# A hybrid attention and Mamba-2 decoder layer: TensorE order written out from the start, products of queries and keys moved inside the attention beats, and 128-row operands in the last SSD chunk

## The chip, the cores and the metric

The kernel runs on one core of a Trainium2 chip. A core has TensorE (PE, matrix products into the PSUM accumulators), VectorE (DVE), ScalarE (ACT) and GpSimd (POOL) for elementwise work, SyncE (SP), which here issues all transfers, and 16 DMA engines. The metric is the device time in microseconds (us) of one execution. A difference under about 0.3% (5.8 us) can't be told from no change here.

## The reference

One layer of a decoder trunk serves a prompt (1 sequence of 1024 tokens) and a sample group (8 sequences of 8 new tokens, with a cache), 1088 tokens in all, in float32.

```python
mod = silu(c) @ w_ada + b_ada                  # shift, scale, gate of each sequence
h = rmsnorm(x, norm_g) * (1 + scale) + shift
q, k, v, g_att, z, xbc, dt, g_a, g_b = split(h @ w_in)
# 3 groups of 8 heads of 64: windows (128, 1), (512, 4), (2048, 16), ALiBi
o_g, lse_g = dilated_attention(q_g, k_g, v_g); att = combine(o_g, lse_g)
y = ssd(silu(conv(xbc)), dt, chunk=128)        # within a sequence: 8 chunks; samples: one of 8 tokens
y = group_rmsnorm((y + d_skip * x) * silu(z))
merged = sigmoid(g_a) * (att * silu(g_att)) @ w_att + sigmoid(g_b) * y @ w_ssm
out = rmsnorm(x + gate * (merged @ w_out))
```

## The kernel before

Activations are stored transposed: 128 features in the partitions, the 1088 tokens in the free dimension, 8 such tiles for the 1024 features. Products with `w_in` are made in three passes (`whi` with `h_hi`, `wlo` with `h_hi`, `whi` with `h_lo`), each in token chunks of 368, 368 and 352. The products of attention and SSD are plain float32, which the trace shows as two records for each matmul; a transpose is one record.

**The opening stage** (pool `ph0`). `xT` is loaded and squared; `sums` adds the squares over the partitions on TensorE, `rms` turns them into reciprocal roots, and four small matmuls `rb` spread these over all partitions. `ada(q)`, for q = 0 to 3, loads two blocks `wa` of `w_ada` (1 MB each), multiplies them with the conditioning vector (L316, four column blocks of 32), copies the result to `row` (ScalarE, L318), transposes it (`adaT`, L320) and makes from it the scale and shift `mod` of the feature tiles 2q and 2q+1 (VectorE, L327 to L329). `modulate(f)` then makes `h_hi[f]` and `h_lo[f]`: for the prompt's 1024 columns VectorE L338, ScalarE L339, VectorE L341; for the 64 sample columns GpSimd L335 to L337, ScalarE L340, GpSimd L342. The first two projections (keys and queries of the first head pair, `early`) are made tile by tile as `h` comes: `passes` goes over two feature tiles at a time, first the two passes with `h_hi`, then that with `h_lo`.

In this stage a planner orders every engine's queue by program order and by its own estimate of when things are ready. From `region` on (behind this stage) TensorE's queue is kept in program order (`manual_schedule`), and the other engines' queues are still the planner's.

**The attention stage.** While the projections `pj` run on, `Order` counts TensorE's time and lets in pieces of attention when they are due. `prompt_group` handles one of 12 pairs (hp = 0 to 3, g = 0 to 2) in beats. A beat i has up to three parts on TensorE: `values(i-2)` (tile `o`, values times transposed weights, 128 rows by 64 columns of the array), `turned(i-1)` (tile `pt`, transposes of the weights `pr`, all of the array), and `scores(i)` (tile `s`, queries times keys, 64 rows by 128 columns). Behind the scores, VectorE (L617) adds the mask and takes the maximum and ScalarE (L620) makes the exponents, both in `pr`, of which there is one buffer. For g = 0 and 1 there are 4 blocks (nb = 4), for g = 2 there are 2:

```python
for i in range(nb + 2):
    if i > 1:
        values(i - 2)
    if 0 < i <= nb:
        turned(i - 1)
    if i < nb:
        scores(i)
```

**The SSD stage** works in the same manner beside the other projections. In `x_tile` the tile `yd` holds the products within a chunk; the ninth chunk (c = 8) has the 64 sample tokens, and its matmuls read 64 rows of `xdt` and of the decay tile `mt` (L1075). The rows 64 to 127 of `mt` for these columns are products with rows of `CB` that are set to zero (L933).

Of the kernel before, what the change touches and what calls it, by code (L numbers as in the profile page):

```python
# [18 lines left out]
NB = 8  # L19
# [91 lines left out]
def trunk(ctx: ExitStack, tc: tile.TileContext, I, O):  # L111
# [36 lines left out]
    def P(name):  # L148
        a, n = PACK[name]
        return pack[:, a:a + n]  # L150
# [73 lines left out]
            SP.dma_start(out=o, in_=i)  # L224
        del copies[:n]

    def passes():

        for ks in (range(i, i + 2) for i in range(0, KO, 2)):
            for k in ks:  # L230
                yield k, 0, 0
                yield k, 1, 0
            for k in ks:
                yield k, 0, 1

    def project_early(js, ws, banks):

        ps = [[b[i](f"early{n}") for i in range(3)] for n, b in enumerate(banks)]
        for k, a, b in passes():
            for w, p in zip(ws, ps):  # L240
                for (c0, cn), q in zip(CHUNKS, p):
                    PE.matmul(q[:, :cn], w[a][:, k, :], (h_hi, h_lo)[b][k][:, c0:c0 + cn], start=(k, a, b) == (0, 0, 0),
                              stop=(k, a, b) == (KO - 1, 0, 1))
        for j, p in zip(js, ps):
            early[j] = p

    loaded = {}

# [40 lines left out]
        return I["w_in"][j]  # L289


    with pool("ph0", 2) as p0:
        xT = [p0.tile([128, TT], F32, name=f"xT{k}", bufs=1) for k in range(KO)]
        cT = p0.tile([128, 8, 9], F32, name="cT", bufs=1)
        SP.dma_start(out=cT, in_=I["cT"])
        for k in range(KO):
            SP.dma_start(out=xT[k], in_=I["xT"][k])
        SP.dma_start(out=pack, in_=I["pack"])
        cth = p0.tile([128, 8, 9], F32, name="cth", bufs=1)
        S.activation(cth, cT, AF.Tanh, scale=0.5)  # L300
        V.scalar_tensor_tensor(cth, cth, 1.0, cT, op0=OP.add, op1=OP.mult)
        V.tensor_scalar_mul(scT[:, :, :9], cth, 0.5)
        mod = p0.tile([128, 2, 8, 9], F32, name="mod", bufs=1)
        bs = p0.tile([128, 8], F32, name="bs", bufs=1)
        V.tensor_scalar_add(bs, P("b_ada")[:, 8:], 1.0)

        def ada(q):

            pr = bankB("ada")
            for k in range(0, 8, 4):  # L310
                wa = p0.tile([128, 4, 4, 128], F32, tag="wa", name="wa", bufs=6)
                SP.dma_start(out=wa.rearrange("p k j n -> p k (j n)"),
                             in_=I["w_ada"][q, k:k + 4].rearrange("k p n -> p k n"))
                for i in range(4):
                    for j in range(4):
                        PE.matmul(pr[j * 32:j * 32 + 32, :128], scT[:, k + i, :], wa[:, i, j, :], start=k + i == 0, stop=k + i == 7)  # L316
            row = p0.tile([128, 128], F32, tag="row", name="row")
            S.activation(row, pr[:, :128], AF.Copy)  # L318
            pt = bankB("adaT")
            PE.transpose(pt[:, :128], row, ident)  # L320
            fs = slice(2 * q, 2 * q + 2)
            pt = pt[:, :128].rearrange("p (i c n) -> p i c n", i=2, c=2)

            def each(ap):
                return ap[:, fs, None].to_broadcast([128, 2, 9])

            V.tensor_tensor(mod[:, 1, fs, :], pt[:, 1, :, :9], each(bs), op=OP.add)  # L327
            V.tensor_tensor(mod[:, 1, fs, :], mod[:, 1, fs, :], each(P("norm_g")), op=OP.mult)
            V.tensor_tensor(mod[:, 0, fs, :], pt[:, 0, :, :9], each(P("b_ada")), op=OP.add)  # L329

        def modulate(f):
            h = xT[f]
            hs = h[:, T:].rearrange("p (b s) -> p b s", b=NB)
            shift = mod[:, 0, f, 0:1]
            G.tensor_tensor(h[:, T:], h[:, T:], rb[:, T:], op=OP.mult)  # L335
            G.tensor_tensor(hs, hs, mod[:, 1, f, 1:, None].to_broadcast([128, NB, NS]), op=OP.mult)
            G.tensor_tensor(hs, hs, mod[:, 0, f, 1:, None].to_broadcast([128, NB, NS]), op=OP.add)  # L337
            V.scalar_tensor_tensor(h[:, :T], h[:, :T], mod[:, 1, f, 0:1], rb[:, :T], op0=OP.mult, op1=OP.mult)  # L338
            S.activation(h_hi[f][:, :T], h[:, :T], AF.Identity, bias=shift)  # L339
            S.activation(h_hi[f][:, T:], h[:, T:], AF.Copy)  # L340
            V.scalar_tensor_tensor(h_lo[f][:, :T], h[:, :T], shift, h_hi[f][:, :T].bitcast(F32), op0=OP.add, op1=OP.subtract)  # L341
            G.tensor_tensor(h_lo[f][:, T:], h[:, T:], h_hi[f][:, T:].bitcast(F32), op=OP.subtract)  # L342

        with tc.high_priority():
            ps = bankA("ms")
            for k in range(KO):
                s2 = p0.tile([128, TT], F32, tag="sqk", name="sqk")
                S.activation(s2, xT[k], AF.Square)
                sums(ps, s2, k == 0, k == KO - 1)
            ms = p0.tile([128, 3, QT], F32, name="ms", bufs=1)  # L350
            rms(ms, ps, D)
            rb = p0.tile([128, TT], F32, name="rb", bufs=1)
            for j in range(4):
                ps = (bankPJ if j < 3 else bankC)("rb")
                row = slice(j * 32, j * 32 + 1)
                PE.matmul(ps[:, :QT], onesc[row, :], ms[row, 1, :], start=True, stop=True, tile_position=(j * 32, 0))
                if j % 2:
                    V.tensor_copy(rb[:, j * QT:(j + 1) * QT], ps[:, :QT])
                else:
                    S.activation(rb[:, j * QT:(j + 1) * QT], ps[:, :QT], AF.Copy)  # L360
        js = (J_K, J_Q)
        for q in range(4):
            ada(q)
            if q == 0:
                ws = [load_w(w_in(j), KO, 128, wp, soon=0)[:2] for j in js]
            for f in (2 * q, 2 * q + 1):
                modulate(f)
        project_early(js, ws, ([bankPJ] * 3, [bankA, bankA, bankC]))


    dsk = const.tile([32, 4], F32, name="dsk")
# [106 lines left out]

        return ap.rearrange("p (r i) -> p i r", r=DIL[g])

    region = ctx.enter_context(ExitStack())
    region.enter_context(tc.manual_schedule(engines={mybir.EngineType.PE}))
    with ExitStack() as actx:
        ap_ = actx.enter_context(pool("att", 2))
        a1 = actx.enter_context(pool("att1", 1))
# [104 lines left out]
        def prompt_group(hp, g, n, q, k, v, msk, o):  # L590
# [3 lines left out]
            per = 512 // w  # L594
            nb = 8 // per
            st = ap_.tile([128, 2, 2, 8], F32, tag="st", name="st")
            prs, pTs, pos = {}, {}, {}

            def behind(u):
                return 2 if (g == 0 and u > 0) or (g == 1 and u % 2 == 1) else 1  # L600
# [1 line left out]
            def scores(i):  # L602
                us = range(i * per, i * per + per)

                ps = [bankA("s0"), bankA("s1")]
                for u in us:
                    nkb = behind(u)
                    c0, k0 = (u - us[0]) * w, (u + 1 - nkb) * 128
                    for h in range(2):
                        hs = slice(h * 64, h * 64 + 64)  # L610
                        mm(ps[h][:, c0:c0 + nkb * 128], q[hs, u * 128:(u + 1) * 128], k[hs, k0:k0 + nkb * 128], 110.0 * nkb,
                           start=True, stop=True)
                pr = prs[i] = ap_.tile([128, 2, 512], F32, tag="pr", name="pr", bufs=1)
                for u in us:
                    c0, m = (u - us[0]) * w, behind(u) * 128
                    for h in range(2):
                        V.tensor_tensor_reduce(out=pr[:, h, c0:c0 + m], in0=ps[h][:, c0:c0 + m], in1=msk[:, h, w - m:w],  # L617
                                               scale=-1.0, scalar=3e38, op0=OP.add, op1=OP.min,
                                               accum_out=st[:, 0, h, u:u + 1])
                        S.activation(pr[:, h, c0:c0 + m], pr[:, h, c0:c0 + m], AF.Exp, scale=-1.0,  # L620
                                     bias=st[:, 0, h, u:u + 1], accum_out=st[:, 1, h, u:u + 1])
# [41 lines left out]
            for i in range(nb + 2):  # L663
                if i > 1:
                    values(i - 2)
                if 0 < i <= nb:
                    turned(i - 1)
                if i < nb:
                    scores(i)
                if i == nb - 1:  # L670
                    order.passed.add(("s", n))
                if i <= nb:
# [148 lines left out]
    with ExitStack() as bctx:  # L821
# [136 lines left out]
        def x_tile(gr, xt, Bk, Bs, CB, CT, CS, sq):  # L958
# [108 lines left out]
            for q in range(3):  # L1067
# [4 lines left out]
                for c in range(4 * q, 4 * q + 4 if q < 2 else 9):  # L1072
                    n = 128 if c < 8 else TS
                    for h in range(2):
                        mm(ps[h * 64:h * 64 + 64, (c % 4) * 128:(c % 4) * 128 + n],  # L1075
                           xdt[:n, c, h * 64:h * 64 + 64], mt[h][:n, c * 128:c * 128 + n], 115.0, start=True, stop=True)
                V.tensor_add(u[:, 512 * q:512 * q + w], u[:, 512 * q:512 * q + w], ps[:, :w])
            V.scalar_tensor_tensor(u, u, 0.5, tiles.pop(("z", xt)), op0=OP.mult, op1=OP.mult)
            SP.dma_start(out=u_d[xt], in_=u)
# [278 lines left out]
```

## Time and profile before

| what | value |
|---|---|
| median of 3 runs | 1927.37 us (1922.1 to 1928.04) |
| the profiled execution's own time | 1927.42 us |
| its span, first to last instruction | 1925.6 us |
| TensorE busy | 1866.4 us (97%) |
| VectorE busy | 1065.8 us (55%) |
| ScalarE busy | 644.9 us (33%) |
| GpSimd busy | 326.6 us (17%) |

Busy time counts overlapping instructions once, and a TensorE instruction is shown longer than the next one has to wait for it; so on this engine the starts of instructions are read, and a stretch of unbroken work can still hold lost time. "Idle before" is the time an engine stood still just ahead of an instruction, with what ended it.

### The profile page before, as it was taken

Reading aid. Unit: us, or ns where it says so; the run is one execution under the profiler, and the core shown is the slowest. Engines: PE = TensorE matmul, PEld = TensorE weight load, DVE = VectorE, ACT = ScalarE, POOL = GpSimd, SP = SyncE. Lnnn points to the kernel's source line nnn. Section 1 sums busy time; section 2 is a strip of 40 time slices with the busy share of each in tenths; the row PEclk is TensorE's granted clock in tenths of the full one; section 3 lists DMA queues with packets and bytes.
Section 4 is the critical chain, followed back from the end, with each engine's and each line's share of the span. In section 5 each row is a group of like instructions: output and inputs, shape, how many; then the busy total and the mean of one; then the engine's idle time right before and its main releaser. Section 6 shows DMA issues by size and latency. Waiting matters only on the chain.

```text
span 1925.6 us, 31964 instructions
## 1 busy us (share of the span) xinstructions
PE 1866.4 (97%) x13057; PEld 1742.9 (91%) x13057; DVE 1065.8 (55%) x1950; ACT 644.9 (33%) x1255; POOL 326.6 (17%) x356
## 2 busy tenths in 40 slices
PE   6999999999999999999999999999999999999998
PEld 4999989988998998999989899989999899999987
DVE  4633343334324323577767676767679755566654
ACT  4434234314432332424342335333533331131222
POOL 3100010010001001132314232423242300000400
PEclk8999999999999999999999999999999999999999
DMA  8422462273246227534443443343334463354322
GB/s 328 138 79 92 158 200 84 89 222 112 96 161 192 84 89 240 154 120 165 146 139 115 170 155 130 119 154 128 92 103 127 147 202 105 132 195 153 118 88 77
DMA packets 108947, 269.54 MB, mean 140 GB/s; under 512 B 41581, under 2 KB 50593, under 8 KB 105537
## 3 DMA queue, kind: packets, MB, share of 16 engines
q1 hardware_dynamic: 108800, 267.51, 42.4%
q8 instruction: 102, 1.67, 0.4%
q14 instruction: 45, 0.36, 0.1%
HBM read 224.93 MB, written 80.26 MB: 158 GB/s over the span
## 4 chain that ended last, share of the span: by engine, by line
PE 41%; DVE 8%; DMA 5%; issue 3%; ACT 3%; POOL 0%; SPq 0%; ACTq 0%; DVEq 0%
PE pj L198 10%; PE pj L199 10%; PE pj L200 10%; DMA csb<-cs_d 4%; PE yd L207 2%; PE fo L1195 2%; PE fo L1193 2%; PE fo L1194 2%; PE yo L207 2%; DMA yx<-u_d 1%; DVE csb L965 1%; DVE xc L869 1%; DVE csb L973 1%; PE sts L207 1%; PE stt L207 1%
## 5 line engine op out<-in xcount | busy, mean ns | idle before, releaser
L198 PE MATMUL pj<-h_hi,whi 128*128 128x368 f32 x2256 | 754.0, 334 | 5.7 <-DVE zs L886 4.6
L200 PE MATMUL pj<-h_lo,whi 128*128 128x368 f32 x2256 | 737.7, 327 | 0.0
L199 PE MATMUL pj<-h_hi,wlo 128*128 128x368 f32 x2256 | 737.5, 327 | 0.0
L198 PEld LDWEIGHTS pj<-h_hi,whi 128*128 128x128 f32 x2256 | 423.9, 188 | 32.8 <-issue 22.8
L199 PEld LDWEIGHTS pj<-h_hi,wlo 128*128 128x128 f32 x2256 | 424.1, 188 | 0.8
L200 PEld LDWEIGHTS pj<-h_lo,whi 128*128 128x128 f32 x2256 | 423.7, 188 | 0.0
L192 DVE TENSOR_TENSOR wlo<-wraw,whi 128x1024 fp32r<-128x1024 f32 (+1 forms) x136 | 163.2, 1200 | 236.1 <-ACT whi L191 221.8
L191 ACT ACTIVATE whi<-wraw 128x1024 fp32r<-128x1024 f32 (+1 forms) x136 | 126.4, 930 | 381.7 <-PE pj L200 365.6
L198 PE MATMUL pj<-yhi,whi 128*128 128x368 f32 (+1 forms) x480 | 157.6, 328 | 2.1 <-DVE acc L1157 2.1
L199 PE MATMUL pj<-yhi,wlo 128*128 128x368 f32 (+1 forms) x480 | 157.4, 328 | 0.0
L200 PE MATMUL pj<-ylo,whi 128*128 128x368 f32 (+1 forms) x480 | 157.1, 327 | 0.0
L620 ACT ACTIVATE pr<-pr,st 128x128 f32<-128x128 f32 (+1 forms) x192 | 83.9, 438 | 88.2 <-DVE st L617 88.1
L198 PEld LDWEIGHTS pj<-yhi,whi 128*128 128x128 f32 x480 | 90.1, 188 | 4.3 <-DVE acc L1157 3.0
L199 PEld LDWEIGHTS pj<-yhi,wlo 128*128 128x128 f32 x480 | 90.1, 188 | 2.1 <-issue 2.1
L200 PEld LDWEIGHTS pj<-ylo,whi 128*128 128x128 f32 x480 | 90.1, 188 | 0.0
L639 DVE COPY pT<-pt 128x512 f32<-128x512 f32 x40 | 27.6, 689 | 102.3 <-ACT pT L641 40.4
L869 DVE SCALAR_TENSOR_TENSOR xc<-raw,cw,xc 128x1112 f32<-128x1112 f32 x60 | 81.9, 1365 | 3.1 <-ACT xc L867 2.2
L965 DVE TENSOR_TENSOR csb<-tok,csb 128x2048 f32<-128x2048 f32 x16 | 46.0, 2877 | 47.8 <-DMA csb<-cs_d 47.8
L500 DVE COPY k<-pj 128x368 f32<-128x368 f32 (+2 forms) x44 | 24.1, 583 | 81.3 <-PE pj L200 79.8
L1162 POOL TENSOR_TENSOR acc<-acc,ta 128x368 f32<-128x368 f32 (+1 forms) x24 | 24.2, 1010 | 263.0 <-DVE ta L1161 262.7
L852 ACT ACTIVATE raw<-pj 128x368 f32<-128x368 f32 (+1 forms) x72 | 31.8, 447 | 87.3 <-PE pj L200 87.3
L1021 DVE SCALAR_TENSOR_TENSOR sta<-sta,eall,stt 128x64 f32<-128x64 f32 x224 | 45.3, 273 | 26.6 <-ACT sta L1017 26.4
(268 smaller groups left out, 2534.8 us busy)
## 6 DMA issues: line engine op xcount, KB each, us to landing
wraw<-in_w_in SPq DMA_DIRECT2D x96, 512.0 KB
csb<-cs_d SPq DMA_DIRECT2D x16, 1088.0 KB
kt<-in_kc SPq DMA_DIRECT2D x32, 448.0 KB
out_kc<-in_kc SPq DMA_DIRECT2D x32, 448.0 KB
out_vc<-in_vc SPq DMA_DIRECT2D x28, 512.0 KB
vt<-in_vc SPq DMA_DIRECT2D x28, 512.0 KB
sg_d<-sg SPq DMA_DIRECT2D x16, 544.0 KB
ecs<-cs_d SPq DMA_DIRECT2D x32, 272.0 KB
```

The lines of the kernel that those rows point to most:

```text
L191: S.activation(hi, raw, AF.Copy)
L192: V.tensor_sub(lo, raw, hi.bitcast(F32))
L198: PE.matmul(ps, whi[:, k, :], xhi[k], start=first and k == 0, stop=False)
L199: PE.matmul(ps, wlo[:, k, :], xhi[k], start=False, stop=False)
L200: PE.matmul(ps, whi[:, k, :], xlo[k], start=False, stop=last and k == n - 1)
L207: PE.matmul(out, w, x, **kw)
L620: S.activation(pr[:, h, c0:c0 + m], pr[:, h, c0:c0 + m], AF.Exp, scale=-1.0, bias=st[:, 0, h, u:u + 1], accum_out=st[:, 1, h, u:u + 1])
L869: V.scalar_tensor_tensor(c, raw[:, t:t + CONV], cw[:, j, t:t + 1], c, op0=OP.mult, op1=OP.add)
L965: V.tensor_tensor(csb[:, :, :T].rearrange("p h (c l) -> p h c l", l=CH), tok[:, :8, 32 + h0:34 + h0].rearrange("p c h -> p h c")[:, :, :, ...
L1021: V.scalar_tensor_tensor(sta[:, i, hs], sta[:, i - 1, hs], eall[:, h0 + h, i:i + 1], ps[:, c, hs], op0=OP.mult, op1=OP.add)
L1193: PE.matmul(ps, hi, whi[:, k, cs], start=k == 0, stop=False)
L1194: PE.matmul(ps, lo, whi[:, k, cs], start=False, stop=False)
```

## The change

Three edits. (1) `region` opens ahead of the opening stage, so TensorE follows program order there too, and that order is written out: `project_early` becomes `early_blocks`, whose `steps(q)` gives 12 blocks of three matmuls for the feature tiles 2q and 2q+1, and `ada` becomes a generator whose five steps (loads; first half of its matmuls; second half; `row`; `adaT` and `mod`) are called in between: for q+1 behind the blocks 3, 6, 7 and 9 of q. All four `rb` copies go to ScalarE, the weights of the first two projections are split behind them, and in `modulate` GpSimd multiplies by the scale ahead of the reciprocal root. (2) In each beat the scores come between the values and the transposes; masks and exponents (`exponents`) stay behind the transposes' copies. (3) The sample chunk's `yd` matmuls read all 128 rows.

```diff
+        def steps(q):
+            ks = (2 * q, 2 * q + 1)
+            for part in [(k, a, 0) for k in ks for a in range(2)] + [(k, 0, 1) for k in ks]:
+                for w, p in zip(ws, ps):
+                    yield lambda w=w, p=p, part=part: block(w, p, *part)
...
+    region = ctx.enter_context(ExitStack())
+    region.enter_context(tc.manual_schedule(engines={mybir.EngineType.PE}))
     with pool("ph0", 2) as p0:
...
+            G.tensor_tensor(hs, hs, mod[:, 1, f, 1:, None].to_broadcast([128, NB, NS]), op=OP.mult)
             G.tensor_tensor(h[:, T:], h[:, T:], rb[:, T:], op=OP.mult)
-            G.tensor_tensor(hs, hs, mod[:, 1, f, 1:, None].to_broadcast([128, NB, NS]), op=OP.mult)
...
+        mods = [ada(q) for q in range(4)]
+        for _ in range(4):
+            next(mods[0])
         js = (J_K, J_Q)
+        wraw = [wp.tile([128, KO, 128], F32, tag="wraw", name="wraw", bufs=3) for _ in js]
+        for j, raw in zip(js, wraw):
+            SP.dma_start(out=raw, in_=w_in(j))
+        rb = p0.tile([128, TT], F32, name="rb", bufs=1)
+        for j in range(4):
+            ps = (bankPJ if j < 3 else bankC)("rb")
+            row = slice(j * 32, j * 32 + 1)
+            PE.matmul(ps[:, :QT], onesc[row, :], ms[row, 1, :], start=True, stop=True, tile_position=(j * 32, 0))
+            last = S.activation(rb[:, j * QT:(j + 1) * QT], ps[:, :QT], AF.Copy)
+        next(mods[0])
+        ws = []
+        with tc.issue_after(last.ins):
+            for raw in wraw:
...
+                S.activation(hi, raw, AF.Copy)
+                V.tensor_sub(lo, raw, hi.bitcast(F32))
...
+        steps = early_blocks(js, ws, ([bankPJ] * 3, [bankA, bankA, bankC]))
+        for m in mods[1:]:
+            next(m)
         for q in range(4):
-            ada(q)
-            if q == 0:
-                ws = [load_w(w_in(j), KO, 128, wp, soon=0)[:2] for j in js]
             for f in (2 * q, 2 * q + 1):
                 modulate(f)
-        project_early(js, ws, ([bankPJ] * 3, [bankA, bankA, bankC]))
+            for n, step in enumerate(steps(q)):
+                step()
+
+                if q < 3 and n in (3, 6, 7, 9):
+                    next(mods[q + 1])
...
                 if i > 1:
                     values(i - 2)
+
+                if i < nb:
+                    scores(i)
                 if 0 < i <= nb:
                     turned(i - 1)
                 if i < nb:
-                    scores(i)
+                    exponents(i)
...
-                           xdt[:n, c, h * 64:h * 64 + 64], mt[h][:n, c * 128:c * 128 + n], 115.0, start=True, stop=True)
+                           xdt[:, c, h * 64:h * 64 + 64], mt[h][:, c * 128:c * 128 + n], 115.0, start=True, stop=True)
```

## Rows read from the trace of the kernel before

**Rows 1.** Page, section 1: busy time, share, instructions of each engine.

```profile
PE 1866.4 (97%) x13057; PEld 1742.9 (91%) x13057; DVE 1065.8 (55%) x1950; ACT 644.9 (33%) x1255; POOL 326.6 (17%) x356
```

**Rows 2.** Windows: stretch, length, busy us per engine, granted clock, DMA share, GB/s.

```profile
18.70:35.80 17.10, 11.97 (x140) 9.13 (x130) 11.18 (x16) 5.82 (x10) 7.67 (x14) 0.50 1.05 392
1288.50:1291.90 3.40, 3.40 (x16) 3.40 (x15) 3.37 (x7) 0.00 (x0) 0.61 (x2) 0.50 0.38 101
```

**Rows 3.** Timeline of TensorE, opening stage: start, length, instruction, idle before.

```profile
22.67 1.29 PE L356 MATMUL rb<-ms,onesc 1*128 1x272 f32 x8
23.89 0.47 PE L320 MATMUL adaT<-pack,row 128*128 128x128 f32 x1
...
30.31 1.93 PE L316 MATMUL ada<-wa,scT 128*32 128x128 f32 x32 [0.69 <-DMA wa<-in_w_ada]
32.17 1.59 PE L242 MATMUL early<-h_hi,whi 128*128 128x368 f32 x4
...
37.09 0.27 PE L320 MATMUL adaT<-pack,row 128*128 128x128 f32 x1
37.29 1.95 PE L316 MATMUL ada<-wa,scT 128*32 128x128 f32 x64
...
42.27 1.25 PE L242 MATMUL early<-h_hi,whi 128*128 128x368 f32 x6
...
62.97 0.36 PE L207 MATMUL dt<-h_hi,dtw 128*64 128x368 f32 x1
```

**Rows 4.** Timeline of ScalarE, opening stage.

```profile
24.86 1.06 ACT L191 ACTIVATE whi<-wraw 128x1024 fp32r<-128x1024 f32 x1 [1.59 <-DMA wraw<-in_w_in]
25.83 0.67 ACT L360 ACTIVATE rb<-rb 128x272 f32<-128x272 f32 x2
29.75 2.41 ACT L339 ACTIVATE h_hi<-xT,mod 128x1024 fp32r<-128x1024 f32 x2 [3.26 <-DVE xT L338]
...
40.67 0.51 ACT L340 ACTIVATE h_hi<-xT 128x64 fp32r<-128x64 f32 x2 [4.96 <-POOL xT L337]
41.08 1.14 ACT L339 ACTIVATE h_hi<-xT,mod 128x1024 fp32r<-128x1024 f32 x1
```

**Rows 5.** Timeline of VectorE, opening stage.

```profile
27.10 0.78 DVE L358 COPY rb<-rb 128x272 f32<-128x272 f32 x2
...
37.82 2.66 DVE L338 SCALAR_TENSOR_TENSOR xT<-xT,mod,rb 128x1024 f32<-128x1024 f32 x2
```

**Rows 6.** Timeline of GpSimd, opening stage.

```profile
37.87 1.53 POOL L336 TENSOR_TENSOR xT<-xT,mod 128x64 f32<-128x64 f32 x2 [1.90 <-DVE mod L328]
39.36 1.52 POOL L337 TENSOR_TENSOR xT<-xT,mod 128x64 f32<-128x64 f32 x2
```

**Rows 7.** Timeline of TensorE in one three-part beat.

```profile
109.87 1.14 PE L207 MATMUL o<-pT,v 128*64 128x128 f32 x16
110.95 1.09 PE L211 MATMUL pt<-pack,pr 128*128 128x128 f32 x8
111.97 1.13 PE L207 MATMUL s<-k,q 64*128 64x256 f32 x8
113.03 0.43 PE L198 MATMUL pj<-h_hi,whi 128*128 128x368 f32 x1
```

**Rows 8.** Timeline of TensorE, a beat without scores.

```profile
120.13 1.09 PE L211 MATMUL pt<-pack,pr 128*128 128x128 f32 x8
120.98 0.41 PE L198 MATMUL pj<-h_hi,whi 128*128 128x368 f32 x1
```

**Rows 9.** Waits of TensorE: what waited, for what, us, times, longest.

```profile
PE tt L211 <- DVE xc L876: 10.0, 7, 3.5
...
PE pj L198 <- DVE zs L886: 4.6, 5, 2.4
...
PE pt L211 <- ACT pr L620: 1.0, 2, 0.5
```

**Rows 10.** Timeline of TensorE, the sample chunk of SSD.

```profile
856.21 0.33 PE L207 MATMUL yd<-csb,xdt 64*64 64x64 f32 x4
```

More of the change, by code (lines that the diff above doesn't have):

```diff
@@ L225, in copy_some, with early_blocks, block @@
         del copies[:n]
[L227 to L236, printed above, removed]
-        ps = [[b[i](f"early{n}") for i in range(3)] for n, b in enumerate(banks)]
[L239 to L243, printed above, removed]
+    def early_blocks(js, ws, banks):
+        ps = [[b[i](f"early{n}") for i in range(3)] for n, b in enumerate(banks)]
+        def block(w, p, k, a, b):
+            for (c0, cn), q in zip(CHUNKS, p):
+                PE.matmul(q[:, :cn], w[a][:, k, :], (h_hi, h_lo)[b][k][:, c0:c0 + cn], start=(k, a, b) == (0, 0, 0),
+                          stop=(k, a, b) == (KO - 1, 0, 1))
         for j, p in zip(js, ps):
             early[j] = p
+        def steps(q):
[3 more added lines that the diff above has]
+                    yield lambda w=w, p=p, part=part: block(w, p, *part)
+        return steps
     loaded = {}
@@ L307, in ada @@
         def ada(q):
-            pr = bankB("ada")
+            was = []
             for k in range(0, 8, 4):
@@ L313, in ada @@
                              in_=I["w_ada"][q, k:k + 4].rearrange("k p n -> p k n"))
+                was.append(wa)
+            yield
+            pr = bankB("ada")
+            for k, wa in zip((0, 4), was):
                 for i in range(4):
@@ L316, in ada @@
                         PE.matmul(pr[j * 32:j * 32 + 32, :128], scT[:, k + i, :], wa[:, i, j, :], start=k + i == 0, stop=k + i == 7)
+                yield
             row = p0.tile([128, 128], F32, tag="row", name="row")
             S.activation(row, pr[:, :128], AF.Copy)
+            yield
             pt = bankB("adaT")
@@ L329, in ada @@
             V.tensor_tensor(mod[:, 0, fs, :], pt[:, 0, :, :9], each(P("b_ada")), op=OP.add)
+            yield
         def modulate(f):
@@ L351, in trunk @@
             rms(ms, ps, D)
[L352 to L360, printed above, removed]
-        js = (J_K, J_Q)
+        mods = [ada(q) for q in range(4)]
+        for _ in range(4):
+            next(mods[0])
+        js = (J_K, J_Q)
+        wraw = [wp.tile([128, KO, 128], F32, tag="wraw", name="wraw", bufs=3) for _ in js]
[11 more added lines that the diff above has]
+            for raw in wraw:
+                hi = wp.tile([128, KO, 128], F32R, tag="whi", name="whi")
+                lo = wp.tile([128, KO, 128], F32R, tag="wlo", name="wlo")
+                S.activation(hi, raw, AF.Copy)
+                V.tensor_sub(lo, raw, hi.bitcast(F32))
+                ws.append((hi, lo))
+        steps = early_blocks(js, ws, ([bankPJ] * 3, [bankA, bankA, bankC]))
+        for m in mods[1:]:
+            next(m)
         for q in range(4):
-            ada(q)
-            if q == 0:
-                ws = [load_w(w_in(j), KO, 128, wp, soon=0)[:2] for j in js]
             for f in (2 * q, 2 * q + 1):
                 modulate(f)
-        project_early(js, ws, ([bankPJ] * 3, [bankA, bankA, bankC]))
+            for n, step in enumerate(steps(q)):
+                step()
+                if q < 3 and n in (3, 6, 7, 9):
+                    next(mods[q + 1])
     dsk = const.tile([32, 4], F32, name="dsk")
@@ L479, in group_view @@
         return ap.rearrange("p (r i) -> p i r", r=DIL[g])
-    region = ctx.enter_context(ExitStack())
-    region.enter_context(tc.manual_schedule(engines={mybir.EngineType.PE}))
     with ExitStack() as actx:
@@ L596, in prompt_group @@
             st = ap_.tile([128, 2, 2, 8], F32, tag="st", name="st")
-            prs, pTs, pos = {}, {}, {}
+            sps, prs, pTs, pos = {}, {}, {}, {}
             def behind(u):
@@ L603, in scores @@
                 us = range(i * per, i * per + per)
-                ps = [bankA("s0"), bankA("s1")]
+                ps = sps[i] = [bankA("s0"), bankA("s1")]
                 for u in us:
@@ L612, in scores, with exponents @@
                            start=True, stop=True)
+            def exponents(i):
+                us = range(i * per, i * per + per)
+                ps = sps.pop(i)
                 pr = prs[i] = ap_.tile([128, 2, 512], F32, tag="pr", name="pr", bufs=1)
```

## The prediction

> **What bounds the kernel.** I read the page first: TensorE is busy 97% of the span [rows 1], so only time on TensorE counts, and the 3% idle is too small to hold a large gain. Then I read TensorE's own timeline in the three places that the diff touches. In the opening stage, the first `early` matmul starts at 32.17 and the next stage (`dt`) at 62.97, with no idle time noted between [rows 3]. So from 32.17 on the old order kept TensorE supplied. The windows add that TensorE had half its clock (0.50 granted) until 35.8 [rows 2]. In the attention stage one beat has no idle time either, but the starts tell more than the busy time does: the same eight transposes take 1.02 us from their start to the next work where scores follow (110.95 to 111.97) and 0.85 where a projection follows (120.13 to 120.98) [rows 7, 8]. Last, the waits of TensorE [rows 9]: those in the attention stage are short; the longer ones are in SSD, behind VectorE.
>
> **The sum is made against 1927.4**, the profiled execution's own time; the median of the runs shown is the same to 0.1 us.
>
> **Edit 1, the start of `early`.** The order up to `rb` (22.67) and the first `adaT` (23.89) stays as it is [rows 3]. What made `early` late came behind: two of the `rb` copies sat on VectorE behind a weight split and ended at 27.88 [rows 5]; ScalarE's first `h_hi` waited for that until 29.75, and TensorE meanwhile did both halves of `ada(1)` up to 32.17 [rows 3, 4]. After: `rb`'s matmuls end at 23.96, ScalarE makes four copies of 0.34, so it is through between 24.3 and 24.7; I take 24.7. Then `whi` twice, 1.06 each, to 26.8, and `h_hi[0]` of 1.2 to 28.0 [rows 4]. VectorE's L338 for tile 0 (1.33 [rows 5]) fits beside `whi`. TensorE starts `early` at about 28.1: **-4.0** (bounds -5.0, if `h_hi[0]` slips between the two `whi`, to -3.4).
>
> What it did in the gap now has to be done later. `ada(1)` was 1.93 us a half at half clock; at full clock a whole `ada` takes 1.95 [rows 3]. With its transpose that is **+2.2**. Each of the three `ada` is now cut in two with blocks between; a further entry and exit of the narrow-column form costs about as much as the entry from `adaT` to `ada` (0.20, 37.09 to 37.29 [rows 3]) and the extra of a beat's switch (0.17): 0.3 x 3 = **+0.9**.
>
> The clock: full speed came at 35.8, 5.5 us after the start of the last unbroken stretch at 30.31 [rows 2, 3]; so 3.6 us of `early` ran at half speed. If it takes 5.5 us again, 5.5 instead of 3.6 us are slow: **+0.9** (bounds 0 and +1.9). Up to here edit 1 comes to 0.0. The transfers cost nothing: SyncE issues them in the order of before (`ada(0)`, two weight tiles, then `ada(1)` to `ada(3)`), `ada(1)`'s second half was there at 30.31 [rows 3] and is wanted behind block 6, after 33, and the later ones have longer still. On ScalarE the two `whi` move behind the `rb` copies, which is in the 28.1 already.
>
> **Edit 1, the joints.** Here is what I think decides. `adaT(q+1)` now stands behind block 9 of q, and the program order leaves blocks 10 and 11 between it and the first block that needs `h_hi[2q+2]`. Six matmuls are about 1.0 us (six in 1.25 with the tail of the last [rows 3]). The way from `adaT` to that `h_hi` is: `adaT` at 37.09, L338 at 37.82 after the three `mod` instructions, its first half 1.33, then L339 1.14 [rows 3 to 5]: 3.25 us at least. Before, the planner put `adaT` early: `adaT` at 37.09, first use of the tiles at 42.27, 5.2 us later, with other blocks between [rows 3]. After, TensorE may not take other blocks. So it stands still 2.2 us at least, at each of three joints. The third chunk of a block also needs the sample columns: GpSimd now has six instructions for two tiles behind `mod`, not four, because the scale comes first and the product with the root can't be made ahead. They take 0.76 each while VectorE runs L338 (37.87 to 40.9 for four [rows 6]). If the fifth ends at about 41.0, L340 adds 0.26, and the third chunk can go 4.2 us after `adaT`; 1.0 + 0.33 of that is covered: **2.9 us a joint**. That is what I take, three times: **+8.7**. Lower bound 3 x 2.2 = +6.6. Upper bound: before, ScalarE had both L340 (40.67) queued ahead of L339 (41.08), and these waited for GpSimd [rows 4]; the same order with six GpSimd instructions gives `h_hi` 5.9 us behind `adaT`: 3 x 4.9 = +14.7.
>
> Whether the standstills cost clock too: before, a wait of 3.5 us for `tt` [rows 9] was followed by 3.4 us at 0.50 [rows 2], and one of 2.4 us [rows 9] wasn't. I take no loss at 2.9 us. [...]
>
> Edit 1 in all: **+8.7** (+4.7 to +16).
>
> **Edit 2.** A three-part beat goes from projection to `o` to `pt` to `s` to projection: 1.08 from `o` to `pt`, 1.02, then 1.06 [rows 7]. Each change of the part of the array in use costs some 0.1 to 0.2 us. After: `o` 1.08, `s` 1.06, `pt` 0.85 as where a projection follows [rows 8]: -0.17. The loops give i = 2 and 3 of g = 0 and 1, so 4 a head pair, 16 beats: **-2.7**. The other 12 beats with scores and transposes begin and end at a projection either way. The row alone would save there too: 28 x 0.17 = 4.8. [...] No row shows scores directly behind a projection in these beats, so the trace doesn't decide.
>
> In the beats with i = 1, TensorE waited twice for the exponents, 1.0 us in all [rows 9]; the scores now come first and cover that: **-1.0**. Against it: VectorE's masks write `pr`, which has one buffer, so they now follow the transposes and the 0.7 us copy behind them. About 0.7 us later, in beats planned 5.5 us apart (the beats of [rows 7, 8] are 9 us apart): hidden. Without that cover it would be 0.7 x 28 = +20, but TensorE's only waits for `pr` in all these beats are the 1.0 us. Edit 2: **-3.7** (0, if the gain is eaten, to -6).
>
> **Edit 3.** Four records, 0.33 us [rows 10], 16 times. The array has the same columns and the stream the same 64 columns; no switch is saved, since it stands apart from the other `yd` and begins behind a projection. The rows 64 to 127 are there already, so nothing new is waited for. **0** (bounds -0.8 and +0.8, 0.05 a time).
>
> **Sum:** 8.7 - 3.7 + 0 = +5.0, so **1932.4 us**. Later stages are limited by TensorE or by waits that shift with it, so nothing gives the opening's loss back.
>
> **Rivals.**
>
> *GpSimd ahead on ScalarE (slower).* If the planner again queues the sample columns' L340 ahead of L339, a joint stands 4.3 to 4.9 us [rows 4, 6]: 12.9 to 14.7, less 3.7: +9.2 to +11, 1937 to 1938. For: it did so in q = 1 to 3 before. Against: at q = 0, with more on GpSimd, L339 went first (29.75).
>
> *The joints cost clock.* 2.9 us a joint and half speed for 3.4 us behind each: 3 x 1.7 more, +10.1, 1937.5. For: the 3.5 us wait. Against: that of 2.4.
>
> *VectorE's order in SSD is drawn anew (faster).* The planner orders the other engines by its own times, which edits 1 and 2 shift. The waits for `xc` and `zs` are 14.6 us [rows 9]. It decides from 10.8 us recovered on (5.0 + 5.8); 12 recovered gives 1920. For: the single waits of 3.5 and 2.4 us stand out. Against: the SSD code's order is the same.
>
> *Edit 2 does nothing* (the change of array form costs as much between `s` and `pt` as it did): +8.7 or, with the 1.0, +7.7, 1935.
>
> **Chances.** Forecast's case (1928 to 1935) 0.47; GpSimd ahead 0.25; clock 0.08; edit 2 nothing 0.08; SSD faster 0.12. 0.3% is 5.8 us. Of the forecast's case three quarters lie within it, a quarter above; of SSD's nine tenths below, a small part within; of the others a small part within, where the joints stand the minimum. Faster 0.11, same 0.43, slower 0.46. The likeliest case's own time is 1932.4; the range 1921 to 1941 takes in the two slower rivals and most of the faster one.
>
> **What would show it.** Right: TensorE's first `early` at 27 to 29; three waits of `early` for `h_hi` of 2 to 5 us each, just behind `adaT`; `dt` starting at 68 to 74 instead of 62.97; transposes of 0.85 us in three-part beats, no waits for `pr`; `yd` of 64 columns as long as before. Wrong: no waits at the joints (then the opening is no later and the kernel faster by 3 to 4 us), half clock far beyond 34 us, or waits of `o` for `pT` in the beats.

## The result, and the profile after

The changed kernel takes 1942.42 us (median of 4 runs, 1939.14 to 1949.04) against 1927.03 us for the kernel before: ratio 1.009, 95% interval 1.0069 to 1.0111, so 15.4 us more. The forecast was 1932.4 (1921 to 1941): the direction of its sum and the place were right, the size was not.

The profiled execution is the slowest of the four (1949.04, span 1947.2). TensorE's busy time in section 1 of the page rose by 8.8 us where the span rose by 21.6, against [rows 1]:

```profile
PE 1875.2 (96%) x13057; PEld 1752.3 (90%) x13057; DVE 1061.7 (55%) x1948; ACT 646.7 (33%) x1257; POOL 334.7 (17%) x356
```

TensorE's timeline in the opening stage answers to [rows 3] (start, length, instruction, idle before):

```profile
27.57 0.98 PE L233 MATMUL early<-h_hi,whi 128*128 128x368 f32 x2 [4.00 <-ACT h_hi L348]
...
37.62 0.27 PE L328 MATMUL adaT<-pack,row 128*128 128x128 f32 x1
37.64 1.24 PE L233 MATMUL early<-h_lo,whi 128*128 128x368 f32 x6
41.01 0.60 PE L233 MATMUL early<-h_hi,whi 128*128 128x368 f32 x2 [2.13 <-ACT h_hi L348]
43.04 1.57 PE L233 MATMUL early<-h_hi,whi 128*128 128x352 f32 x4 [1.43 <-ACT h_hi L349]
...
54.96 0.61 PE L233 MATMUL early<-h_hi,whi 128*128 128x368 f32 x2 [2.13 <-ACT h_hi L348]
57.00 1.57 PE L233 MATMUL early<-h_hi,whi 128*128 128x352 f32 x4 [1.43 <-ACT h_hi L349]
...
70.30 0.60 PE L233 MATMUL early<-h_hi,whi 128*128 128x368 f32 x2 [2.12 <-ACT h_hi L348]
72.34 0.93 PE L233 MATMUL early<-h_hi,whi 128*128 128x352 f32 x4 [1.43 <-ACT h_hi L349]
...
80.07 0.35 PE L207 MATMUL dt<-h_hi,dtw 128*64 128x368 f32 x1 [0.30 <-DVE dtw L413]
```

`early` starts 4.6 us sooner than before, and yet `dt` starts 17.1 us later (80.07 against 62.97). At each of the three joints (the places where the first tiles of the next `q` are wanted) there are the six covering matmuls behind `adaT` (37.64), then two waits: 2.13 us for the tile's prompt columns, and, after two matmuls, 1.43 us for its sample columns. That is 10.7 us for three.

The windows of the same trace show the second loss, in the granted clock (the 0.50 behind the busy times of the five engines), against [rows 2]:

```profile
36.00:42.60 6.60, 3.48 (x22) 2.85 (x18) 4.31 (x6) 1.43 (x2) 4.21 (x5) 1.00 1.04 391
42.70:46.10 3.40, 3.06 (x10) 2.92 (x10) 1.28 (x1) 1.55 (x3) 0.85 (x4) 0.50 0.07 27
46.20:56.20 10.00, 7.24 (x92) 5.91 (x91) 4.29 (x6) 1.43 (x2) 3.85 (x4) 1.00 0.00 0
56.40:63.10 6.70, 6.10 (x45) 5.23 (x46) 1.28 (x1) 1.55 (x3) 1.11 (x5) 0.50 0.17 43
73.40:76.80 3.40, 3.40 (x14) 3.40 (x13) 1.28 (x1) 0.49 (x2) 0.60 (x2) 0.50 0.80 255
```

Behind each joint TensorE runs at half its clock for 3.4, 6.7 and 3.4 us, in which it works for 12.6 us; by estimate half of that, 6.3 us, is lost (e4 below puts it to the test).

Why the joint is longer than forecast is on GpSimd, VectorE and ScalarE, timelines of the first joint, GpSimd's instructions one by one, against [rows 4 to 6]:

```profile
38.39 0.30 POOL L344 TENSOR_TENSOR xT<-xT,mod 128x64 f32<-128x64 f32 x1 [7.02 <-DVE mod L336]
38.65 1.27 POOL L344 TENSOR_TENSOR xT<-xT,mod 128x64 f32<-128x64 f32 x1
39.89 1.29 POOL L345 TENSOR_TENSOR xT<-xT,rb 128x64 f32<-128x64 f32 x1
41.15 1.30 POOL L345 TENSOR_TENSOR xT<-xT,rb 128x64 f32<-128x64 f32 x1
42.41 0.29 POOL L346 TENSOR_TENSOR xT<-xT,mod 128x64 f32<-128x64 f32 x1
```

```profile
38.35 2.66 DVE L347 SCALAR_TENSOR_TENSOR xT<-xT,mod,rb 128x1024 f32<-128x1024 f32 x2
40.99 1.28 DVE L350 SCALAR_TENSOR_TENSOR h_lo<-xT,mod,h_hi 128x1024 fp32r<-128x1024 f32 x1
```

```profile
39.81 1.15 ACT L348 ACTIVATE h_hi<-xT,mod 128x1024 fp32r<-128x1024 f32 x1 [3.37 <-DVE xT L347]
42.73 0.51 ACT L349 ACTIVATE h_hi<-xT 128x64 fp32r<-128x64 f32 x2 [1.78 <-POOL xT L346]
43.15 1.13 ACT L348 ACTIVATE h_hi<-xT,mod 128x1024 fp32r<-128x1024 f32 x1
```

The planner did put ScalarE's prompt columns of the first tile (39.81) ahead of the sample columns, as the forecast's case has it. But the sample columns came 5.1 us behind `adaT` (42.73 against 37.62), not 3.9, because GpSimd's fifth instruction ended only at 42.70. Three of the five took 1.27 to 1.30 us, and each of these lasted until 0.15 to 0.18 us behind the end of one of VectorE's instructions: two of L347, then `h_lo` (L350), which began at 40.99 right behind them. Before the change `h_lo` (L341) began only at 42.25, and of GpSimd's four instructions two were long and two short, as these two show:

```profile
37.87 0.30 POOL L336 TENSOR_TENSOR xT<-xT,mod 128x64 f32<-128x64 f32 x1 [1.90 <-DVE mod L328]
38.12 1.27 POOL L336 TENSOR_TENSOR xT<-xT,mod 128x64 f32<-128x64 f32 x1
```

So the 0.76 us that the forecast took as GpSimd's price in [rows 6] is the mean of a short one and a long one.

A three-part beat and the sample chunk's products, timeline of TensorE, against [rows 7, 8 and 10]:

```profile
126.36 1.14 PE L207 MATMUL o<-pT,v 128*64 128x128 f32 x16
127.44 1.13 PE L207 MATMUL s<-k,q 64*128 64x256 f32 x8
128.50 1.09 PE L211 MATMUL pt<-pack,pr 128*128 128x128 f32 x8
129.35 0.41 PE L198 MATMUL pj<-h_hi,whi 128*128 128x368 f32 x1
...
871.71 0.34 PE L207 MATMUL yd<-csb,xdt 128*64 128x64 f32 x4
```

From `o` to the projection it is 2.99 us instead of 3.16, with the parts as forecast (1.08, 1.06, 0.85). The waits of `pt` for `pr` are gone from TensorE's list. The sample chunk takes 0.34 us instead of 0.33.

### The profile page after: what moved, and what is told of

The parts are those of the page before. It is cut to its first block, busy times and chain, and to the rows that moved or that the text cites. A ratio compares the mean times of both kernels' runs of the same rounds, so it can differ in the third digit from the quotient of the medians.

```text
span 1947.2 us, 32002 instructions
## 1 busy us (share of the span) xinstructions
PE 1875.2 (96%) x13057; PEld 1752.3 (90%) x13057; DVE 1061.7 (55%) x1948; ACT 646.7 (33%) x1257; POOL 334.7 (17%) x356
## 4 chain that ended last, share of the span: by engine, by line
PE 80%; DVE 7%; DMA 6%; ACT 3%; issue 3%; POOL 1%; SPq 0%; ACTq 0%; DVEq 0%; POOLq 0%
PE pj L198 20%; PE pj L199 19%; PE pj L200 19%; DMA csb<-cs_d 4%; PE s L207 2%; PE o L207 2%; PE pt L211 2%; PE yd L207 2%; PE fo L1224 2%; PE fo L1225 2%; PE fo L1226 2%; PE yo L207 2%; PE early L233 1%; DVE csb L1003 1%; DVE wlo L192 1%
```

## The experiments

Each was timed beside the kernel before on the same chip. "dt" is the start of the `dt` matmuls in the profiled execution, the end of the opening stage.

| run | ratio to before, 95% interval | median us | dt us |
|---|---|---|---|
| changed kernel | 1.009 (1.0069 to 1.0111) | 1942.4 | 80.07 |
| e2_opening: edit 1 alone | 1.008 (1.0066 to 1.0095) | 1941.8 | 80.18 |
| e1_beats: edit 2 alone | 0.9992 (0.9977 to 1.0008) | 1923.5 | 61.99 |
| e1b_beats: again | 0.9973 (0.9957 to 0.9989) | 1922.4 | 62.96 |
| e3_rows: edit 3 alone | 1.002 (1.0006 to 1.0034) | 1927.5 | 61.97 |
| e3b_rows: again | 1.000 (0.9985 to 1.0015) | 1927.6 | 61.71 |
| c_before: the kernel before | 1.0004 (0.9986 to 1.0022) | 1927.5 | 61.94 |
| e4_fill: changed, joints filled | 1.0021 (1.0011 to 1.0031) | 1929.7 | 76.00 |
| e5_early: `adaT` behind block 3 | 0.9998 (0.9981 to 1.0014) | 1926.9 | 65.24 |
| e6_ahead: `ada` further ahead | 0.9973 (0.9955 to 0.999) | 1921.6 | 63.76 |
| e7_root: GpSimd's order as before | 1.0081 (1.0058 to 1.0105) | 1944.8 | 85.43 |
| e8_late: `adaT` behind block 11 | 1.0069 (1.0043 to 1.0094) | 1942.1 | 83.50 |
| e9_ahead_64: e6 without edit 3 | 0.9973 (0.9954 to 0.9992) | 1922.3 | 62.28 |

**Which edit loses: e2, e1, e3.** Each is the kernel before with that edit of the diff alone.

> Only edit 1 (the written-out opening) on the kernel before. Theory J: dt starts at about 80 us instead of 63, so 1944 us (+17). Rival B: the opening loses less than its shift, because later stages take part of it up, and edit 2 or 3 loses the rest: 1935 us or less.

Edit 1 alone costs 1.008 and brings `dt` to 80.18: the loss is all its own. Its waits at the joints are 2.12 and 1.43 us again, and its clock is at 0.50 behind each.

> Only edit 2 (scores between values and transposes) on the kernel before. Theory J (all of the loss is in the opening: three joints where TensorE waits for h_hi, and the half clock that follows them): this run gains 4 to 5 us, 1922 to 1923 us; a three-part beat takes about 0.19 us less from projection to projection (3.69 to 3.50), twelve beats with scores and transposes alone 0.04 to 0.06 less, and the two waits for pr (1.0 us) are gone. Rival B (masks and exponents behind the transposes hold something up later): 1927 us or more, with waits of TensorE for pr or pT that the kernel before lacks.

The beat came out as in the changed kernel: 2.99 us from `o` (108.30) to the projection (111.29). No wait for `pr` or `pT` is in its list. But the time, 0.9992, didn't settle it: its interval touches both theories.

> Only edit 3 (128 rows in the sample chunk) on the kernel before. Theory J: no change, 1927 us within 2; the yd beats of the sample chunk 0.80 and 1.72 us from projection to projection as before. Rival R (the longer operands cost a wait or a switch in SSD, where the changed kernel's profile is also later): 1930 us or more.

1.002, with an interval that leaves out 1, spoke for rival R, though no stage of the trace was longer. So both went once more, beside a control:

> The kernel before, unchanged, as a control: what the comparison makes of no change. Theory N (the spread of the later stages, from run to run, is what blurs edits 2 and 3): a ratio within 0.998 to 1.002, so that 1.002 for edit 3 alone and 0.999 for edit 2 alone can't be told from their expected 1.000 and 0.998. Rival (the comparison is finer than that): 1.000 within 0.0005.

> Edit 2 alone once more. Theory J: the beats save 4 to 5 us (counted in the first run's trace), so 0.998 and below the control. Rival B: 1.000 or more, the saving is given back later.

> Edit 3 alone once more. Theory N: 1.000 within 0.002, the stage of the sample chunk's products as long as before. Rival R (the 128-row operands cost some 2 to 4 us somewhere in SSD): again 1.001 to 1.003, and above the control.

The control shows an interval 0.0018 wide to each side with nothing changed (3.5 us). Edit 3 is at 1.000 now: the 1.002 did not repeat. Edit 2 is at 0.9973, 5.2 us less, with an interval that leaves out 1; with the 0.9992 of its first run the mean is 0.998 (3.4 us), as theory J has it. Rival B has no support in the traces or in this run; in the first run alone it could not be told from theory J.

**The clock by itself: e4.** The changed kernel with matmuls in the waits:

```diff
+        def fill(q, n):
+            for _ in range(n):
+                PE.matmul(q[:, :368], ws[0][0][:, 0, :], h_hi[0][:, :368], start=True, stop=True)
-        def block(w, p, k, a, b):
+        def block(w, p, k, a, b, joint=None):
+            if joint:
+                fill(joint, 13)
             for (c0, cn), q in zip(CHUNKS, p):
+                if joint and c0 == 736:
+                    fill(joint, 9)
...
```

`joint` is a spare accumulator at the first block of q = 1, 2 and 3. The results of these matmuls are not used.

> The changed kernel with matmuls that compute nothing needed (368 columns into a spare accumulator), 13 ahead of the first block and 9 ahead of its third chunk at each of the three joints, so that TensorE is busy while it waits for h_hi. They take 2.2 and 1.5 us, as long as the waits (2.1 and 1.4). Theory J with the clock as a part of the price: no half clock behind the joints, dt at about 73 us instead of 80, 1935 to 1936 us. Rival W (the waits alone are the price, the clock costs nothing): dt at 80 us or later, 1942 us.

Its timeline at the first joint and its windows:

```profile
40.62 2.33 PE L233 MATMUL fill<-h_hi,whi 128*128 128x368 f32 x13
42.91 0.60 PE L241 MATMUL early<-h_hi,whi 128*128 128x368 f32 x2
43.34 1.66 PE L233 MATMUL fill<-h_hi,whi 128*128 128x368 f32 x9
44.95 0.93 PE L241 MATMUL early<-h_hi,whi 128*128 128x352 f32 x4
```

```profile
36.00:79.00 43.00, 43.00 (x376) 38.47 (x376) 20.42 (x28) 12.49 (x23) 17.79 (x28) 1.00 0.41 145
```

The joint is 0.2 us longer than without the fill (4.3 us from the fill's start to the third chunk, against 4.2 from the start of the wait at 38.88 to 43.04), and the clock stays at 1.00. From the first `early` to `dt` it is 47.3 us (28.69 to 76.00) instead of 52.5 (27.57 to 80.07): 5.2 us less, though TensorE has more to do, so this was the clock's. The longer joints hide 0.5 us of it. This run was also slower to reach full clock at first (the first half of `ada(1)` still takes 1.90 us at 33.38; in the changed kernel it takes 1.15 at 32.23), which by estimate hides some 0.8 more (the second half starts at 36.90 instead of 35.01, 1.9 us later, of which 1.1 are the later start of `early`); together 6.5, beside the 6.3 read from the windows. `dt` came at 76 instead of the 73 expected: the expectation left these two and the later start of `early` (1.1 us) out. The whole kernel gained 12.7 us by its medians, and the opening only 4.1: the other 8.6 are not explained.

**The cover: e8 and e5.** Only the list of blocks behind which `ada(q+1)` goes on:

```diff
-                if q < 3 and n in (3, 6, 7, 9):
+                if q < 3 and n in (3, 6, 7, 11):     # e8_late
+                if q < 3 and n in (0, 1, 2, 3):      # e5_early
```

> The changed kernel with adaT behind block 11 instead of 9, so with no block between it and the first use. Theory J: the first wait of each joint grows by the cover taken away, 1.0 us, to 3.1 us, the second stays 1.4; dt at 83 us or, with a longer half clock, 85; 1945 to 1948 us. Rival W: no change, 1942 us.

> The changed kernel with ada(q+1) behind the blocks 0, 1, 2 and 3 of q instead of 3, 6, 7 and 9, so that eight blocks (4.0 us) stand between adaT and the first use of its tiles instead of two. Theory J (the joints are a matter of cover: h_hi 3.4 us behind adaT, its sample columns 5.4): the first wait of each joint is gone, the second is about 1.0 us; no half clock behind the joints; dt at 65 to 67 us instead of 80, 1927 to 1930 us. Rival W (the waits come from somewhere else, as from late weights or transfers, and move with the order): waits of 2 us and more stay, 1935 us or more.

In e8 the first wait is 3.12 us instead of 2.13 and the second 1.44; in e5 only one wait of 0.86 is left (TensorE's timelines, e8 and then e5):

```profile
41.95 0.60 PE L233 MATMUL early<-h_hi,whi 128*128 128x368 f32 x2 [3.12 <-ACT h_hi L348]
43.99 0.66 PE L233 MATMUL early<-h_hi,whi 128*128 128x352 f32 x1 [1.44 <-ACT h_hi L349]
```

```profile
38.81 0.49 PE L233 MATMUL early<-h_hi,whi 128*128 128x368 f32 x2
40.17 0.42 PE L233 MATMUL early<-h_hi,whi 128*128 128x352 f32 x1 [0.86 <-ACT h_hi L349]
```

Two blocks less cover are 1.0 us more wait, as theory J has it, and `dt` moved to 83.50 and 65.24. In e5 the clock stayed at 1.00 from 36 to 62. The total of e8 (1942.1) missed its 1945 to 1948: the 3.4 us by which its `dt` is later don't show in its median of four runs, which lie between 1936.1 and 1951.4.

**GpSimd's part: e7.** The two products with scale and root in the order of before:

```diff
+            G.tensor_tensor(h[:, T:], h[:, T:], rb[:, T:], op=OP.mult)
             G.tensor_tensor(hs, hs, mod[:, 1, f, 1:, None].to_broadcast([128, NB, NS]), op=OP.mult)
-            G.tensor_tensor(h[:, T:], h[:, T:], rb[:, T:], op=OP.mult)
```

> The changed kernel with GpSimd's product with the root ahead of that with the scale again, as before the change, so that the root's products can be made ahead and four GpSimd instructions stand behind mod instead of six. Theory G (a good part of a joint is GpSimd): the second wait of each joint (1.4 us) goes; ScalarE may then queue L349 ahead of L348 as before, which makes the first wait 3.5 to 4 instead of 2.1; a joint is 2.1 to 4.1 us instead of 3.6, dt at 76 to 82. Rival (ScalarE's path alone decides): first wait 2.1 and second wait 1.4 as they are.

TensorE's waits between 16 and 90 us:

```profile
PE early L233 <- ACT h_hi L348: 15.6, 4, 3.9
PE early L233 <- ACT h_hi L349: 5.4, 1, 5.4
```

The joint became one wait of 3.9 us, since ScalarE queued the sample columns first, and the very first block waited 5.4 us for GpSimd, which made all the root's products first. `dt` came at 85.43, outside the expected 76 to 82: I had left that first block out. So in the opening the diff's order of the two products is worth 5.4 us of `dt` with this place of `adaT`; the whole kernel's time doesn't show it (1.0081 and 1.009, with intervals that overlap).

**Versions without joints: e6 and e9.**

```diff
+        ahead = {(0, n): 1 for n in (1, 3, 4, 5)} | {(0, n): 2 for n in (9, 10, 11)} | {(1, 1): 2}
+        ahead |= {(1, n): 3 for n in (8, 9, 10)} | {(2, 0): 3}
...
-                if q < 3 and n in (3, 6, 7, 9):
-                    next(mods[q + 1])
+                if (q, n) in ahead:
+                    next(mods[ahead[q, n]])
```

> The changed kernel with ada running further ahead: ada(1) behind the blocks 1, 3, 4, 5 of q = 0, the first three steps of ada(2) behind its blocks 9, 10, 11 and its adaT behind block 1 of q = 1, ada(3) behind blocks 8, 9, 10 of q = 1 with adaT behind block 0 of q = 2. Theory J: no wait of over 0.5 us at any joint, full clock from about 35 us on, dt at 62 to 64 us, as early as before the change; with edit 2's gain 1921 to 1924 us, below the kernel before. Rival W: dt at 68 us or later.

> The version with ada running ahead (no joints), edit 2 kept, edit 3 taken back (64 rows in the sample chunk). Theory N: the same as with edit 3, 0.997, about 1922 us. Rival R: 2 to 4 us faster than that, 0.995 to 0.996.

All of TensorE's waits in e6 between 16 and 90 us:

```profile
PE early L233 <- ACT h_hi L348: 3.9, 1, 3.9
PE ada L322 <- DMA wa<-in_w_ada: 1.9, 2, 1.2
PE early L233 <- ACT h_hi L349: 0.4, 1, 0.4
PE ms L165 <- ACT sqk L357: 0.2, 1, 0.2
PE adaT L328 <- ACT row L325: 0.2, 1, 0.2
```

No joint is left (the waits for `h_hi` are ahead of the first block). Both versions are at 0.9973, faster than the kernel before; e9 without edit 3 is the same, so rival R isn't seen here either. But edit 2 alone is at 0.9992 and 0.9973, and `dt` at 62.3 to 63.8 is where the planner's own order has it (61.7 to 63.0 in six profiles). The written-out order, done well, brings nothing that these comparisons can tell from edit 2's gain.

## Why the prediction was wrong, by its steps

- **Start of `early`** (28.1, -4.0): 27.57, -4.6. Right; in the eight traces with edit 1 it is 27.5 to 28.7.
- **`ada(1)` inside, the cuts, the first half clock** (2.2 + 0.9 + 0.9 = +4.0): what remains of 17.1 after the other terms is 17.1 + 4.6 - 10.7 - 6.3 = 4.7. Right to 0.7, as a sum; it wasn't taken apart, and it holds two waits that the forecast didn't have, 0.38 for the first sample columns and 0.30 for `dtw`.
- **The joints** (three, 2.9 us each, +8.7): the mechanism was right, and e8 and e5 moved it by the cover. The size was 3.56, +10.7. The term that was too small is GpSimd's, and it was so within the forecast's own sum: at 0.76 each, five instructions from 37.87 end at 41.67, not at "about 41.0", which gives 3.5 a joint and +10.5. In the trace the five took 4.31 (38.39 to 42.70), 0.86 each; three of them ended only 0.15 to 0.18 us behind the end of an instruction of VectorE, and the mean of [rows 6] hid that.
- **"I take no loss at 2.9 us"**: this step failed. The clock fell at all three joints, 6.3 us by the trace, 5.2 by e4. It was there as a rival, at 0.08, and against it stood a single wait of 2.4 us without loss, which was one draw: the same wait was followed by 0.50 in the changed kernel (last section). And a joint isn't one wait: two, 2.1 and 1.4, with two matmuls between. The trace has 0.50 behind each joint; in e5, with one wait of 0.86 a joint, the clock stayed at 1.00 from 36 to 62. Half speed lasted 3.4, 6.7 and 3.4 us, where the rival had 3.4 each and 5.1 in all.
- **Edit 2** (-3.7): right. By the starts of the projections around them 16 beats save 0.19 us each (0.17 of it between `o` and the projection), 12 beats some 0.05, not 0.17, and the waits 1.0: 4.6 in all. That the 12 beats save nothing, as the 2.7 has it, no run shows; the 0.05 is what the traces have in its place. Timed, -1.5 in the first run and -5.2 in the second.
- **Edit 3** (0): right within what two runs can tell (1.002 and 1.000).
- **The sum**: by measured terms 17.1 - 4.6 = +12.5, timed +15.4. The 3 us between are not explained by an edit. From `dt` to the end the profiled executions took 1850.8 to 1867.1 us with edit 2 (nine kernels, the changed one the longest) and 1855.9 to 1870.3 without it (five): a spread of over 10 us. Waits for `xc` of up to 4.0 us and for `so` of up to 2.6, and half clock behind some of them, come and go from run to run: 3.4 us at 0.50 behind an `xc` wait of 3.54 in the kernel before and behind one of 3.97 in the changed kernel, there also 6.8 and 3.4 us behind `so` waits of 1.84 and 2.14. What decides which run gets them stays open. The rival of a new VectorE order in SSD has no support: by the traces VectorE's instructions there have the order of before but for one pair of neighbours, the transfers have it too, and the waits for `xc` and `zs` are 13.0 us instead of 14.6.

TensorE's waits for these two in the changed kernel, against [rows 9]:

```profile
PE tt L211 <- DVE xc L906: 8.0, 6, 4.0
...
PE pj L198 <- DVE zs L916: 5.0, 5, 2.5
```

## What to carry to other kernels

When a queue is written out by hand, the distance between a producer and its first consumer has to be at least the whole way through the other engines, counted from the trace; two blocks of 0.5 us can't cover 3.4 and 5.4. Where a planner's order shows no idle time, a hand-written one has little to win: the best one here had `dt` at 62.3, the planner's at 61.7 to 63.0. And here a standstill of TensorE cost more than its length (10.7 us of waits and, by estimate, 5.2 to 6.3 us of half clock behind them), so useful work that was ready would have been worth more there than its own time. A mean over a group of instructions can hide two prices; the ones that a forecast rests on are to be read singly.

## What the runs showed of the hardware that was not expected

- The granted clock fell to 0.50 behind each of the six joints of the changed kernel and e2 (waits of 2.1 and 1.4 us). From 36 to 62 us it was 0.82 on average in e8 (first joint 3.1 and 1.4), 0.93 in e7 (waits of 3.9), and 1.00 in e5, where a joint has one wait of 0.86.
- Between these lengths a wait alone didn't settle it. The longest wait for `zs` is 2.45 us in the kernel before (1511.08) and 2.46 in the changed one (1533.05); 0.50 followed in the second, and not in the first. And a wait of 3.29 us for `raw` in the changed kernel (1006.76) was not followed by it (1.00 from 1006.7 to 1020). What decides stays open here; the lines below show the `zs` wait in the kernel before and in the changed one.
- GpSimd's 128 by 64 operations on `xT` in the opening took either 0.29 to 0.34 us or 1.27 to 1.36, and nothing between, in the kernel before and in the changed one: every long one ended 0.15 to 0.18 us behind the end of an instruction of VectorE over 128 by 1024.
- The same kernel against itself differed by up to 15.7 us between single runs (1919.61 to 1935.29), and edit 2 alone came out at 0.9992 and at 0.9973; so an effect of 0.2% can't be read from one comparison.

```profile
1511.08 0.43 PE L198 MATMUL pj<-h_hi,whi 128*128 128x352 f32 x1 [2.45 <-DVE zs L886]
1511.20:1514.50 3.30, 3.30 (x21) 3.30 (x22) 3.25 (x7) 1.83 (x5) 0.00 (x0) 1.00 0.51 159
```

```profile
1533.05 0.43 PE L198 MATMUL pj<-h_hi,whi 128*128 128x352 f32 x1 [2.46 <-DVE zs L916]
1534.40:1537.60 3.20, 3.20 (x13) 3.20 (x12) 3.20 (x13) 0.60 (x2) 0.00 (x0) 0.50 0.28 105
```
